# Output projection and gate of a decoder layer: tokens on partitions, seven half-size products, PSUM seeded by VectorE

## The chip, the cores and the metric

The kernel runs on one core of a Trainium2 chip. Its engines work side by side, each through its own queue in order: TensorE (PE, matrix products into PSUM), VectorE (DVE), ScalarE (ACT), GpSimd (POOL), and SyncE (SP), which issues all of this kernel's DMAs. The metric is the device time in microseconds, median of several runs. A profile is one execution, taken by the hardware profiler.

## The reference

One layer over 4096 tokens of 1024 channels, in f32. What is cut away here (convolution, spatial gating) is not touched by the change.

```python
h = _layer_norm(x, ln_emb_g, ln_emb_b)
proj = einsum("bsd,de->bse", h, w_in)                  # 6 parts of 512 channels
y_a = ...  # a = a_val*sigmoid(a_gate); causal depthwise conv of width 31;
           # silu(layer_norm(a)) * silu(a_z)
y_b = ...  # gelu(b_u) * (chunked 128x128 mix of layer_norm(gelu(b_v)) + b_s) * silu(b_z)
y = concatenate([y_a, y_b], axis=-1)                   # 1024 channels
mix = einsum("bse,ed->bsd", y, w_out)                  # output projection
h = _layer_norm(ALPHA * h + mix, post_ln_g, post_ln_b)
pe = einsum("bsk,kd->bsd", p, w_ple)                   # 256 -> 1024
gate = sigmoid(einsum("bsd,de->bse", h, w_ple_gate) + b_ple_gate)
h = h + gate * pe
```

Every f32 product is done in three passes of the fast 32-bit matmul format: an operand is split into a rounded part (hi, by ScalarE) and the rest (lo = source - hi, by VectorE or GpSimd), and hi*hi + lo*hi + hi*lo are summed in PSUM (`mm3`, L158).

## The kernel before, in words

There are eight blocks of 512 tokens and four stages. Stage 1 normalises x, projects the convolution's inputs and its gate, and runs the convolution of channel tiles 0 and 1 on VectorE (`conv`, 31 multiply-adds per tile, L205). Stage 2 (L488) projects the gating branch in three parts of four 128-token tiles per block (L506), mixes it, and runs the convolution of channel tiles 2 and 3 beside it. Intermediate results go to DRAM tensors: `hD` (normalised x), `cD` (convolution), `zD` (silu gate of the first branch), `yD` (second branch).

Stage 3 (L627) is the output projection, with channels on partitions and tokens on the free axis: for each block and each 128 output channels (d), 8 x 3 matmuls of 128x128 by 128x512 go into one PSUM bank (L648). VectorE adds the residual (`zp`, L653), transposes 32x32 pieces and takes moments over channels in groups (L661, L666), which `block_moments` joins through DRAM. `stage_y` (L452) prepares the next block's left side; the eight weights `wO` are split one after the other in stage 2's last block (L554).

Stage 4 (L683) is the gate, in the same layout: `stage_z` (L614) normalises the block's rows, the gate needs 8 x 3 matmuls per 128 output channels (L708), the embedding product 2 x 3 (`embed`, L713), then sigmoid, product, sum and the output's DMA.

Work for later blocks is written as generators (`Background`, L163) from which the loops take a step now and then. The order on each engine is not the written one alone: when the program is built, a scheduler puts every instruction into its engine's queue as soon as its own model of the machine finds its inputs ready, the one written first ahead of others. At run time each queue is strictly in order. Buffers come from pools with a fixed number of tiles under one tag; a tile that is taken again waits for the last user of the old one. All of stages 1 to 4 share the pools `wpool`, `hpool`, `rpool` and `psum` (L60 to L63).

Of the kernel before, what the change touches and what calls it, by code (L numbers as in the profile page):

```python
# [8 lines left out]
F32 = mybir.dt.float32  # L9
# [6 lines left out]
P = 128  # L16
S = 4096
# [17 lines left out]
def hybrid_layer_kernel(  # L35
# [50 lines left out]
    xst = const.tile([P, S // P, 2], F32, name="xst")  # L86
    cw_sb = const.tile([P, CT, W31], F32, name="cw_sb")
# [9 lines left out]
    rD = [dram.tile([KT // 2, P, 2, TB], F32, name=f"rD{b}") for b in range(NB)]  # L97
# [3 lines left out]
    rpD = [dram.tile([4, 32, QT, 12], F32, name=f"rpD{b}") for b in range(NB)]  # L101
    rsD = [dram.tile([32, QT, 2], F32, name=f"rsD{b}") for b in range(NB)]
# [32 lines left out]
    def by_row(eng, dst, src, mr, i):  # L135
        """dst = src - mean (i = 0) or src / deviation (i = 1); tokens on the free axis"""
# [55 lines left out]
    def conv(pairs, dst, part):  # L192
        """pairs: two (channel tile, a tile with its halo) of one block."""
# [29 lines left out]
    # ---------------- phase 1: embedding norm, gate / value / a_z, conv of channel tiles 0, 1  # L223
# [160 lines left out]
    # ---------------- phase 2: b_v, b_u, b_z, spatial gating, conv of channel tiles 2, 3  # L384
# [424 lines left out]
```

## Time and profile before

| | us |
|---|---|
| median of 3 runs (1976.82 to 1980.04) | 1979.33 |
| span of the profiled execution | 1978.5 |
| stage 1, 0 to 569.5 us of the span | 569.5 |
| stage 2, to 1115.9 us | 546.4 |
| stage 3, to 1512.5 us | 396.6 |
| stage 4 | 466.0 |

The span runs from the first to the last instruction; the device time of the profiled execution itself is not listed apart from the runs, whose median lies 0.8 us above the span. The stages are cut where the first matmul of the next one starts (the first with `h_hi`, with `yh`, with `zh`); work of other engines for a later stage may lie before the cut. "Busy" of TensorE counts matmuls, which overlap, so the price of one is read from a stretch without gaps.

### The profile page before, as it was taken

How to read it: one execution, taken by the hardware profiler on the slowest of the kernel's cores; microseconds unless marked ns; L12 is line 12 of the kernel's file. 1: busy time of each engine (PE TensorE's matmuls, PEld its weight loads, DVE VectorE, ACT ScalarE, POOL GpSimd, SP SyncE). 2: the span in 40 equal slices, each digit the busy share in tenths (PEclk: the TensorE clock that was granted, in tenths of full speed). 3: DMA queues.
4: the chain of work that ended last, by engine and by line, in shares of the span. 5: the costliest groups of instructions: out<-in, count | busy, mean ns of one | idle time of the engine just before them, and what ended most of it. 6: DMA issues, size and time to landing. Idle time of an engine off the chain costs nothing.

```text
span 1978.5 us, 23196 instructions
## 1 busy us (share of the span) xinstructions
PE 1892.0 (96%) x8340; PEld 1554.8 (79%) x8340; DVE 1564.5 (79%) x2746; ACT 509.4 (26%) x724; POOL 842.4 (43%) x575
## 2 busy tenths in 40 slices
PE   7999989999999999999999988999897799999999
PEld 6877777878888888888888876778776588888887
DVE  7999998989699999999998576666769766666421
ACT  5323311230332222222222331111202233323321
POOL 1876756461234564655456333332422333323221
PEclk9999999999999999999999999999999899999999
DMA  7644433432321234212223575555535322222111
GB/s 265 210 161 137 153 128 134 126 131 92 130 85 57 68 89 134 67 51 75 66 67 106 169 218 174 175 183 171 173 115 181 120 102 106 101 97 85 59 43 38
DMA packets 176871, 239.44 MB, mean 121 GB/s; under 512 B 21490, under 2 KB 113906, under 8 KB 176756
## 3 DMA queue, kind: packets, MB, share of 16 engines
q1 hardware_dynamic: 176756, 237.96, 37.2%
q8 instruction: 65, 1.06, 0.2%
q14 instruction: 50, 0.41, 0.1%
HBM read 156.55 MB, written 81.36 MB: 120 GB/s over the span
## 4 chain that ended last, share of the span: by engine, by line
PE 55%; DVE 14%; DMA 10%; issue 4%; POOL 3%; ACT 1%; SPq 0%; DVEq 0%; POOLq 0%; ACTq 0%
PE ps L159 11%; PE ps L160 11%; PE ps L161 11%; PE gp L160 5%; PE gp L161 5%; PE gp L159 5%; DVE acc L205 3%; DVE yf L144 2%; DMA zs<-zD 2%; DVE zn L144 2%; PE pp L159 1%; PE pp L161 1%; PE pp L160 1%; DMA rD<-zp 1%; DMA yf<-cD 1%
## 5 line engine op out<-in xcount | busy, mean ns | idle before, releaser
L205 DVE SCALAR_TENSOR_TENSOR acc<-a,cw_sb,acc 128x512 f32<-128x512 f32 x928 | 639.5, 743 | 3.0
L159 PE MATMUL ps<-hh,whi 128*128 128x512 f32 (+1 forms) x784 | 303.7, 390 | 21.0 <-DVE a L336 8.6
L160 PE MATMUL ps<-hl,whi 128*128 128x512 f32 (+1 forms) x784 | 303.8, 388 | 0.8 <-DVE hl L124 0.8
L161 PE MATMUL ps<-hh,wlo 128*128 128x512 f32 (+1 forms) x784 | 303.0, 387 | 0.0
L160 PE MATMUL ps<-wlo,h_hi 128*128 128x512 f32 x768 | 298.9, 389 | 0.0
L159 PE MATMUL ps<-whi,h_hi 128*128 128x512 f32 x768 | 298.9, 389 | 0.0
L161 PE MATMUL ps<-whi,h_lo 128*128 128x512 f32 x768 | 298.8, 389 | 0.0
L696 POOL TENSOR_TENSOR h<-zh,zl 128x512 f32<-128x512 f32 x64 | 116.9, 1830 | 294.7 <-DVE h L727 155.7
L159 PE MATMUL ps<-yh,whi 128*128 128x512 f32 x512 | 205.6, 402 | 31.3 <-DVE zp L653 31.3
L160 PE MATMUL ps<-yl,whi 128*128 128x512 f32 x512 | 203.5, 397 | 0.7 <-POOL yl L124 0.7
L161 PE MATMUL ps<-yh,wlo 128*128 128x512 f32 x512 | 203.4, 397 | 0.0
L160 PE MATMUL gp<-zl,whi 128*128 128x512 f32 x512 | 200.3, 391 | 0.0
L159 PE MATMUL gp<-zh,whi 128*128 128x512 f32 x512 | 200.1, 391 | 0.2 <-DVE zp L653 0.2
L161 PE MATMUL gp<-zh,wlo 128*128 128x512 f32 x512 | 199.7, 390 | 0.0
L159 PEld LDWEIGHTS ps<-hh,whi 128*128 128x128 f32 x784 | 147.6, 189 | 56.5 <-DVE ev L340 10.8
L726 DVE TENSOR_TENSOR sg<-pp,sg 128x512 f32<-128x512 f32 (+1 forms) x65 | 44.3, 683 | 184.2 <-ACT h L700 151.7
L144 POOL TENSOR_TENSOR xk<-xk,mr 128x1024 f32<-128x1024 f32 x42 | 156.7, 3760 | 45.4 <-DMA xk<-in_xT 38.2
L160 PEld LDWEIGHTS ps<-hl,whi 128*128 128x128 f32 x784 | 148.7, 190 | 30.3 <-DVE hl L124 1.2
L161 PEld LDWEIGHTS ps<-hh,wlo 128*128 128x128 f32 x784 | 148.7, 190 | 29.8
L161 PEld LDWEIGHTS ps<-whi,h_lo 128*128 128x128 f32 x768 | 144.2, 188 | 29.8
L159 PEld LDWEIGHTS ps<-whi,h_hi 128*128 128x128 f32 x768 | 144.2, 188 | 29.7
L160 PEld LDWEIGHTS ps<-wlo,h_hi 128*128 128x128 f32 x768 | 144.2, 188 | 29.1
(112 smaller groups left out, 2971.2 us busy)
## 6 DMA issues: line engine op xcount, KB each, us to landing
h_lo<-hD SPq DMA_DIRECT2D x32, 512.0 KB, 3.7
zp<-hD SPq DMA_DIRECT2D x64, 256.0 KB, 3.3
rD<-zp SPq DMA_DIRECT2D x32, 512.0 KB, 4.1
zn<-rD SPq DMA_DIRECT2D x32, 512.0 KB, 4.8
out<-h SPq DMA_DIRECT2D x63, 256.0 KB, 2.0
xt<-in_x SPq DMA_DIRECT2D x28, 512.0 KB, 4.5
xk<-in_xT SPq DMA_DIRECT2D x28, 512.0 KB, 6.4
hD<-xk SPq DMA_DIRECT2D x56, 256.0 KB, 2.5
```

The lines of the kernel that those rows point to most:

```text
L144: eng.tensor_tensor(dst, src, m, op=(ALU.subtract, ALU.mult)[i])
L159: nc.tensor.matmul(ps, lhsT=lh, rhs=rh, start=first, stop=False)
L160: nc.tensor.matmul(ps, lhsT=lh, rhs=rl, start=False, stop=False)
L161: nc.tensor.matmul(ps, lhsT=ll, rhs=rh, start=False, stop=last)
L205: nc.vector.scalar_tensor_tensor(o if t == W31 - 1 else acc, src, w, acc, op0=ALU.mult, op1=ALU.add)
L696: nc.gpsimd.tensor_tensor(h2, zh[e // 2][:, e % 2, :].bitcast(F32), zl[e // 2][:, e % 2, :].bitcast(F32), op=ALU.add,)
L726: nc.vector.tensor_tensor(sg[:, cs], pp[:, cs], sg[:, cs], op=ALU.mult)
```

## The change

Stages 1 and 2 keep their own work. Stages 3 and 4 are written anew, with 128 tokens on partitions and 512 output channels on the free axis, for a pair of 128-token tiles at a time (16 pairs). The left side of a pair is a 2x2 matrix of blocks (two token tiles by two halves of the 1024 inputs), the weight a 2x2 matrix of 512x512 quarters. The 2x2 block product is formed from seven products of sums (Winograd's form of Strassen's scheme) in place of eight. Each product is 4 x 3 matmuls.

The sums on the left (s1 to s4) are made by VectorE in PSUM banks and then split. The sums on the weight's side are made once, beside stages 1 and 2 (`combos`), and kept in the DRAM tensor `twD`. The sums over the products use PSUM's accumulation: several products are added into one bank without starting it anew, and two banks (`pa`, `pd`) are first written by VectorE ("seeded") with an earlier product plus the residual or the bias, and a product is then accumulated on top. `open_banks` runs one matmul with zeros into each of these two banks at the start of stage 3.

The residual alpha*h is prepared beside stage 2 in token layout (`token_rows`, DRAM tensor `hT`). With tokens on partitions the moments of a row are two `bn_stats` and one `bn_aggr`, and ScalarE normalises the row; it goes to DRAM (`zT`), and stage 4 reads it again and transposes it on TensorE (`zn_left`). GpSimd applies gain and offset of the norm to the rows in stage 4. `y_block` prepares a block of the first branch with two of its four channel tiles at a time. Stages 3 and 4 have pools of their own, opened when those of stages 1 and 2 are closed.

```diff
+    psum = p12.enter_context(tc.tile_pool(name="psum", bufs=2, space=PSUM))
...
+    def combos(u, w, scale=None, bias=None):
...
+        for c in range(2):
+            q = {}
+            for i in range(2):
+                for j in range(2):
+                    q[i, j] = b4([P, 2, C], "bq")
+                    dma(q[i, j], w[i, j][:, 2 * c : 2 * c + 2, :])
...
+            for n, ij in ((0, (0, 0)), (1, (1, 0)), (2, (1, 1))):
+                dma(twD[u][n][:, cs, :], q[ij])
+            sub = ALU.subtract
+            nc.gpsimd.tensor_tensor(q[0, 0], q[0, 1], q[0, 0], op=sub)
+            dma(twD[u][4][:, cs, :], q[0, 0])
...
+    def token_rows():
...
+        for tt in range(S // P):
+            xt = b4([P, D], "xrow")
+            dma(xt, x[tt * P : (tt + 1) * P, :])
...
+            nc.gpsimd.tensor_tensor(xt, xt, rows[0], op=ALU.mult)
+            nc.gpsimd.tensor_tensor(xt, xt, rows[1], op=ALU.add)
+            dma(hT[tt], xt)
...
+    bg_row.add(combos(0, wo))
+    bg_row.add(combos(1, wg, dv_sb[:, 2, :], dv_sb[:, 3, :]))
+    bg_row.add(token_rows())
...
+                bg_row.step(1)
-                if b == NB - 1 and part > 0:
-                    d = (part - 1) * JT + j
-                    stg = h4([P, D], "wstg", F32) if part == 1 else q4([P, D], "wstg")
-                    wO[d] = prep_weight(stg, wo[d])
...
+    p12.close()
+    pool = ctx.enter_context(tc.tile_pool(name="p34", bufs=1, reuse_waits="tile"))
+    psum = ctx.enter_context(tc.tile_pool(name="psum34", bufs=1, space=PSUM, reuse_waits="tile"))
...
+    def big(shape, name, dt=F32):
+        return pool.tile(shape, dt, tag="big", name=name, bufs=5)
...
+    def right_operands(u):
+        W = {}
+        for n in ORDER:
+            stg = big([P, 4, C], "wst")
+            dma(stg, twD[u][ROW[n]])
+            hi, lo = wtile("whi"), wtile("wlo")
+            for c in range(2):
+                cs = slice(2 * c, 2 * c + 2)
+                act(hi[:, cs], stg[:, cs], AF.Identity)
+                eng = nc.gpsimd if c else nc.vector
+                eng.tensor_tensor(lo[:, cs], stg[:, cs], hi[:, cs].bitcast(F32), op=SUB)
...
+    def product(ps, n, L, W, start):
+        ah, al = L[n]
+        wh, wl = W[n]
+        kw = dict(skip_group_check=True)
+        for k in range(4):
+            nc.tensor.matmul(ps, lhsT=ah[:, k, :], rhs=wh[:, k, :], start=start and k == 0, stop=False, **kw)
+            nc.tensor.matmul(ps, lhsT=al[:, k, :], rhs=wh[:, k, :], start=False, stop=False, **kw)
+            nc.tensor.matmul(ps, lhsT=ah[:, k, :], rhs=wl[:, k, :], start=False, stop=k == 3, **kw)
...
+    def group(L, W, add11, add12, add21, add22, to12, to22, between):
+        pb = pbank("B", "pb", 2)
+        pe = pbank("E", "pe", 1)
+        product(pb, 1, L, W, True)
+        product(pe, 5, L, W, True)
+        pa = pbank("A", "pa", 1)
+        tt(pa, pb, add11, op=ADD)
+        s5 = utile([P, C], "s5")
+        tt(s5, pe, add22, op=ADD)
+        between(0)
+        product(pb, 6, L, W, False)
+        u2 = utile([P, C], "u2")
+        tt(u2, pb, add12, op=ADD)
+        between(1)
+        product(pe, 3, L, W, False)
+        tt(to12, pe, u2, op=ADD)
+        between(2)
+        product(pb, 7, L, W, False)
+        pd = pbank("D", "pd", 1)
+        tt(pd, pb, add21, op=ADD)
+        tt(to22, pb, s5, op=ADD)
+        between(3)
+        product(pa, 2, L, W, False)
+        between(4)
+        product(pd, 4, L, W, False)
+        between(5)
+        return pa, pd
...
+    def y_block(b):
...
+            by_row(nc.vector, ya[:, us], ya[:, us], mr, 0)
+            by_row(nc.gpsimd, ya[:, us], ya[:, us], mr, 1)
...
+            nc.gpsimd.tensor_tensor(ya[:, us], ya[:, us], zs[:, us], op=ALU.mult)
...
+    def stats(zt, first):
...
+        nc.vector.bn_stats(st[:, 0, :], first)
+        nc.vector.bn_stats(st[:, 1, :], zt[:, C:])
+        nc.vector.bn_aggr(mv[:, 0, :], st)
+        rstd_of(mv)
+        nc.vector.scalar_tensor_tensor(
+            nb, mv[:, 0, 0:1], -1.0, mv[:, 0, 1:2], op0=ALU.mult, op1=ALU.mult
         )
+        for dst, src in ((zt[:, :C], first), (zt[:, C:], zt[:, C:])):
+            act(dst, src, AF.Identity, scale=mv[:, 0, 1:2], bias=nb)
...
+        def between(i):
+            bg.step(2)
+            if i < 2:
+                r = rows[i]
+                nc.gpsimd.tensor_tensor(r, r, gb[:, 0], op=ALU.mult)
+                nc.gpsimd.tensor_tensor(r, r, gb[:, 1], op=ADD)
+            elif i == 3:
+                finish4(0, 1, c12)
+            elif i == 4:
+                finish4(1, 1, c22)
```

In a pair the left operands are made from the blocks a11, a12, a21, a22: s1 = a21 + a22, s2 = s1 - a11, s4 = a12 - s2, s3 = a11 - a21; each is split into `ahi` (ScalarE) and `alo` (VectorE for the four sums, GpSimd for the three plain blocks). `finish4` is sigmoid, embedding product, multiplication, addition and output DMA for half a row tile.

What moves in the queues is shown at three places, each before and after. First GpSimd in a middle block of stage 2. `h_lo` is the rest of the next block's input, `v` and `vl` the normalised value of the gating branch, `mv` its moments, `g` the gated output. Before:

```order
L108 TENSOR_SCALAR mv<-mv 128x1
L124 TENSOR_TENSOR h_lo<-h_lo,h_hi 128x1024
L108 TENSOR_SCALAR mv<-mv 128x1
L109 TENSOR_TENSOR mv<-mv,nhalf 128x1 x2
L521 TENSOR_TENSOR v<-v,sgb 128x512 x2
L108 TENSOR_SCALAR mv<-mv 128x1
L522 TENSOR_TENSOR v<-v,sgb 128x512 x2
```

After, `xrow` being a token row of `token_rows`:

```order
L496 TENSOR_TENSOR xrow<-xrow,hrow 128x1024
L126 TENSOR_TENSOR h_lo<-h_lo,h_hi 128x1024
L495 TENSOR_TENSOR xrow<-xrow,hrow 128x1024
L126 TENSOR_TENSOR h_lo<-h_lo,h_hi 128x1024
L496 TENSOR_TENSOR xrow<-xrow,hrow 128x1024
L495 TENSOR_TENSOR xrow<-xrow,hrow 128x1024
L571 TENSOR_TENSOR g_7310<-g_7310,zz 128x512 x2
L571 TENSOR_TENSOR g_7388<-g_7388,zz 128x512 x2
L496 TENSOR_TENSOR xrow<-xrow,hrow 128x1024
L495 TENSOR_TENSOR xrow<-xrow,hrow 128x1024
L110 TENSOR_SCALAR mv<-mv 128x1
L496 TENSOR_TENSOR xrow<-xrow,hrow 128x1024
```

The token rows stand between the instructions of the gating branch, from block 2 to block 6; in block 1 it is the second set of weight differences. Blocks 0 and 7 of stage 2 have none.

Second, GpSimd where stage 2 ends. Before, the first block's left side (`yf`, `yl`) is mixed with the last gating products:

```order
L470 TENSOR_TENSOR yf<-yf,zs 128x512 [waits DMAHW7_49,Activation_49]
L124 TENSOR_TENSOR yl<-yf,yh 128x512 [waits DMAHW0_49,Activation_49]
L124 TENSOR_TENSOR yl<-yf,yh 128x512 [waits DMAHW1_49,Activation_49]
L534 TENSOR_TENSOR g_8905<-g_8905,zz 128x512 [waits DMAHW3_49,Activation_49]
L124 TENSOR_TENSOR yl<-yf,yh 128x512 [waits DMAHW2_49,PE_49,Activation_49]
L534 TENSOR_TENSOR g_8905<-g_8905,zz 128x512 [waits Activation_49]
```

After, with `g` as above, `zero` the tile of `open_banks`, `ya` the first branch of block 0, `wlo` half a rest of a weight:

```order
L111 TENSOR_TENSOR bmv<-bmv,nhalf 32x16 [waits Pool_49]
L571 TENSOR_TENSOR g_9254<-g_9254,zz 128x512 [waits DMAHW1_49,Activation_49]
L571 TENSOR_TENSOR g_9254<-g_9254,zz 128x512 [waits Activation_49]
L722 MEMSET zero 128x512 [waits PE_49]
L146 TENSOR_TENSOR ya<-ya,mr 128x1024 [waits DMAHW3_49,DMAHW4_49,DVE_49,PE_49]
L146 TENSOR_TENSOR ya<-ya,mr 128x1024 [waits DMAHW5_49,DVE_49]
L784 TENSOR_TENSOR ya<-ya,zs 128x1024 [waits DMAHW6_49,Activation_49,Pool_49]
L784 TENSOR_TENSOR ya<-ya,zs 128x1024 [waits Activation_49,Pool_49]
L659 TENSOR_TENSOR wlo<-wst,whi 128x1024 [waits DMAHW3_49,Activation_49]
L670 TENSOR_TENSOR alo<-ya,ahi 128x512 [waits Activation_49]
```

All of the first block's preparation now stands behind the last product of stage 2, and the first `alo`, which the second matmul of stage 3 waits for, behind a weight's rest.

Third, VectorE in the middle of stage 3. Before, a residual sum frees a bank (`zp`), and transposes, moments and rests of the left side follow:

```order
L653 SCALAR_TENSOR_TENSOR zp<-zp,ps 128x512 [waits PE_49] x2
L661 STREAM_TRANSPOSE zt<-zp 128x512 [waits DVE_49]
L661 STREAM_TRANSPOSE zt<-zp 128x512
L653 SCALAR_TENSOR_TENSOR zp<-zp,ps 128x512 [waits PE_49]
L124 TENSOR_TENSOR yl<-yf,yh 128x512 [waits PE_49,Activation_49]
```

After, from the moments of one row tile to the seeds of the next products (`znb` is -mean/deviation, `pa` and `pd` the seeded banks, `pb` and `pe` the others):

```order
L817 BN_STATS st<-pa 128x6 [waits PE_49]
L819 BN_AGGR zmv<-st 128x2 [waits DVE_49]
L821 SCALAR_TENSOR_TENSOR znb<-zmv 128x1 [waits DVE_49,Pool_49]
L748 TENSOR_TENSOR pd<-pb,row 128x512 [waits PE_49]
L749 TENSOR_TENSOR z_10581<-pb,s_10610 128x512
L735 TENSOR_TENSOR pa<-pb,row 128x512 [waits DMAHW7_49,Activation_49]
L818 BN_STATS st<-z_10581 128x6 [waits DVE_49]
L737 TENSOR_TENSOR s_10772<-pe,row 128x512 [waits DMAHW0_49,PE_49]
```

The seeds now stand behind a VectorE instruction that waits for GpSimd. The order of the products on TensorE in a settled pair is 1, 5, 6, 2, 7, 3, 4.

## Rows read from the trace of the kernel before

**Rows 1.** The page, part 1: busy time, share of the span, instructions
```profile
PE 1892.0 (96%) x8340; PEld 1554.8 (79%) x8340; DVE 1564.5 (79%) x2746; ACT 509.4 (26%) x724; POOL 842.4 (43%) x575
```

**Rows 2.** Windows: length; PE, PEld, DVE, ACT, POOL busy (instructions); clock, DMA share, GB/s
```profile
0.00:569.50 569.50, 538.19 (x2383) 441.34 (x2384) 510.38 (x789) 162.02 (x231) 291.74 (x152) 0.99 0.45 148
569.50:1115.90 546.40, 546.40 (x2501) 456.01 (x2501) 518.87 (x1099) 143.71 (x225) 299.82 (x275) 1.00 0.27 81
1115.90:1512.50 396.60, 364.43 (x1539) 295.08 (x1537) 273.25 (x598) 76.10 (x104) 133.10 (x85) 0.97 0.56 179
1512.50:1978.50 466.00, 442.96 (x1920) 362.38 (x1920) 262.02 (x263) 127.55 (x165) 117.77 (x64) 0.98 0.25 87
1690.00:1960.00 270.00, 270.00 (x1183) 221.57 (x1182) 131.48 (x124) 77.44 (x101) 68.51 (x39) 1.00 0.20 74
```

**Rows 3.** Waits of PE, whole span: in total, times, longest
```profile
PE ps L159 <- DVE zp L653: 31.3, 14, 5.1
PE pp L159 <- ACT ph L123: 13.7, 1, 13.7
```

**Rows 4.** Groups of VectorE by form: busy us, mean ns | idle before
```profile
L144 DVE TENSOR_TENSOR zn<-zn,mr 128x1024 f32<-128x1024 f32 x64 | 133.4, 2121 | 21.8 <-DMA zn<-rD 21.6
L144 DVE TENSOR_TENSOR xk<-xk,mr 128x1024 f32<-128x1024 f32 x14 | 55.7, 3980 | 18.5 <-POOL xk L144 18.5
L726 DVE TENSOR_TENSOR sg<-pp,sg 128x512 f32<-128x512 f32 x63 | 43.5, 691 | 178.3 <-ACT h L700 151.7 <-ACT sg L725 26.6
L124 DVE TENSOR_TENSOR yl<-yf,yh 128x512 fp32r<-128x512 f32 x32 | 25.3, 819 | 33.3 <-ACT yh L123 33.3
L114 DVE BATCH_NORM_STATS2 bst<-v 128x6 f32<-128x512 f32 x32 | 21.7, 679 | 4.2 <-ACT v L516 4.2
L115 DVE BATCH_NORM_AGGREGATE xst<-bst 128x2 f32<-128x12 f32 x32 | 6.4, 200 | 0.1
```

**Rows 5.** Groups of GpSimd by form, the same columns
```profile
L144 POOL TENSOR_TENSOR xk<-xk,mr 128x1024 f32<-128x1024 f32 x42 | 156.7, 3760 | 45.4 <-DMA xk<-in_xT 38.2 <-issue 7.2
L124 POOL TENSOR_TENSOR h_lo<-h_lo,h_hi 128x1024 fp32r<-128x1024 f32 x32 | 77.8, 2433 | 107.1 <-ACT h_hi L123 107.1
L124 POOL TENSOR_TENSOR yl<-yf,yh 128x512 fp32r<-128x512 f32 x32 | 44.2, 1391 | 28.9 <-ACT yh L123 28.8
L109 POOL TENSOR_TENSOR mv<-mv,nhalf 128x1 f32<-128x1 f32 x32 | 18.1, 567 | 1.6
L108 POOL TENSOR_SCALAR mv<-mv 128x1 f32<-128x1 f32 x32 | 8.0, 251 | 33.1 <-DVE mv L115 33.1
```

**Rows 6.** Line 205, convolution: duration min/median/max ns, first and last start
```profile
L205 DVE SCALAR_TENSOR_TENSOR acc<-a,cw_sb,acc x928: 672/745/776, 40.9 to 1068.0; 128x512 f32<-128x512 f32 x186
```

**Rows 7.** PE in order of time, stage 1: start, duration; four transposes
```profile
19.32 0.28 PE L159 MATMUL ps<-hh,whi 128*128 128x256 f32 x1
19.44 0.60 PE L253 MATMUL tp<-ident,xt 128*128 128x128 f32 x4
```

**Rows 8.** A window of the start; GpSimd in order of time, block 1's last rest
```profile
20.00:30.00 10.00, 9.24 (x65) 8.26 (x64) 7.51 (x12) 7.12 (x12) 0.00 (x0) 1.00 1.04 365
...
83.56 2.40 POOL L124 TENSOR_TENSOR hl<-xk,hh 128x1024 fp32r<-128x1024 f32 x1
```

**Rows 9.** GpSimd at the end of stage 2; DMA: count, KB, us to landing
```profile
1120.03 2.93 POOL L109 TENSOR_TENSOR bmv<-bmv,nhalf 32x16 f32<-32x16 f32 x1
1122.94 1.28 POOL L534 TENSOR_TENSOR g<-g,zz 128x512 f32<-128x512 f32 x1
...
wstg<-in_wo SPq DMA_DIRECT2D x8, 512.0 KB, 4.5
mr<-csD SPq DMA_DIRECT2D x8, 512.0 KB, 5.1
```

**Rows 10.** A window behind the wait of stage 4, columns as in rows 2
```profile
1542.00:1546.00 4.00, 3.90 (x9) 3.10 (x10) 4.00 (x6) 0.62 (x2) 0.00 (x0) 0.51 0.61 215
```

**Rows 11.** Tile gp: duration min/median/max ns, first and last start
```profile
L161 PE MATMUL gp<-zh,wlo x512: 388/389/628, 1513.1 to 1973.2; 128*128 128x512 f32 x171
```

More of the change, by code (lines that the diff above doesn't have):

```diff
@@ L414, in cg_prep @@
         ah, al = h4([P, D], "cgh"), h4([P, D], "cgl")
         split(acc, ah, al)
-        for _ in range(8):
+        for _ in range(4):
             yield
@@ new lines, in hybrid_layer_kernel, with zn_left @@
+    Z = {}
+    def zn_left(p, L):
+        Z[p] = load_rows(zT, p)
+        quads = []
+        zq = big([P, 4, 4, P], "zq")
+        for j in range(2):
+            for half in range(2):
+                tp = sbank("tp")
+                for kk in range(4):
+                    k = 4 * half + kk
+                    nc.tensor.transpose(
+                        out=tp[:, kk * P : (kk + 1) * P],
+                        in_=Z[p][j][:, k * P : (k + 1) * P], identity=ident,
+                    )
+                zt = zq[:, 2 * j + half]
+                act(zt, tp.rearrange("p (k x) -> p k x", k=4), AF.Identity)
+                quads.append(zt)
+                yield
+        yield from left_operands(L, *quads, nc.gpsimd)
@@ new lines, in hybrid_layer_kernel @@
+    H = load_rows(hT, 0)
+    for p in range(NP):
+        h1, h2 = H
+        if p + 1 < NP:
+            H = load_rows(hT, p + 1)
+            if p % 2 == 0 and p // 2 + 1 < NB:
+                bg_x.add(y_block(p // 2 + 1))
+            if p % 2 == 1:
+                bg_x.drain()
+            bg.add(left3(p + 1, Lnext))
+        else:
+            bg.add(zn_left(0, Lnext))
+        z1, z2 = ztile([P, D], "z1"), ztile([P, D], "z2")
+        def between(i):
+            bg.step(2)
+            bg_x.step(1)
+        pa, pd = group(
+            L, W, h1[:, :C], h1[:, C:], h2[:, :C], h2[:, C:], z1[:, C:], z2[:, C:], between
+        )
+        stats(z1, pa)
+        dma(zT[2 * p], z1)
+        stats(z2, pd)
+        dma(zT[2 * p + 1], z2)
+        bg.drain()
+        L, Lnext = Lnext, {}
@@ new lines, in hybrid_layer_kernel, with finish4, between @@
+    for p in range(NP):
+        if p + 1 < NP:
+            bg.add(zn_left(p + 1, Lnext))
+        rows = Z.pop(p)
+        ph, pl = p_left(p)
+        c12, c22 = utile([P, C], "c12"), utile([P, C], "c22")
+        def finish4(j, half, src):
+            cs = slice(half * C, (half + 1) * C)
+            sg = c12 if (j, half) == (0, 1) else c22 if (j, half) == (1, 1) else utile([P, C], "sg")
+            act(sg, src, AF.Sigmoid)
+            pp = sbank("pp")
+            ts = slice(j * P, (j + 1) * P)
+            for k in range(2):
+                mm3(
+                    pp, ph[:, k, ts], pl[:, k, ts], wp_hi[:, k, cs], wp_lo[:, k, cs],
+                    k == 0, k == 1,
+                )
+            tt(sg, pp, sg, op=ALU.mult)
+            tt(rows[j][:, cs], rows[j][:, cs], sg, op=ADD)
+            dma(out[2 * p + j][:, cs], rows[j][:, cs])
+        def between(i):
+            bg.step(2)
+            if i < 2:
[6 more added lines that the diff above has]
+                finish4(1, 1, c22)
+        pa, pd = group(L, W, cg[:, :C], cg[:, C:], cg[:, :C], cg[:, C:], c12, c22, between)
+        finish4(0, 0, pa)
+        finish4(1, 0, pd)
+        bg.drain()
+        L, Lnext = Lnext, {}
@@ L737 @@
+_OUT = (S // P, P, D)
 def kernel(**inputs):
```

406 lines of the change are left out of this document (210 added, 196 removed).

## The prediction

> **What bounds the kernel now.** Read the stages first, then the waits of TensorE inside them, then the prices of single instructions. The page gives TensorE 96% of the span, which says only that it is the engine to follow [rows 1]. The windows by stage say more [rows 2]: stage 1 takes 569.5 us and stage 2 546.4 us, and in stage 2 TensorE has no idle time at all, VectorE is 95% busy and GpSimd 55%. Stage 3 takes 396.6 us with TensorE busy 364 us, stage 4 takes 466.0 us with 443 us. A stretch in the middle of stage 4 holds 1183 matmuls in 270 us of unbroken work, so one 128x512 matmul costs 0.228 us when nothing waits. At that price stage 3 (1536 matmuls) is 350 us of work and 46 us of waits and slow clock; stage 4 (1920) is 438 us of work, 5 us behind the last matmul (it starts at 1973.2 us [rows 11]) and 23 us of waits. The named waits are for VectorE's residual sums, which give the accumulators back (31.3 us), and one of 13.7 us at the head of stage 4 [rows 3]. So stages 3 and 4 are bound by TensorE with 69 us of gaps, and stages 1 and 2 share their limit between TensorE and VectorE.
>
> **The change, part by part.** The sum is made against the profiled execution, span 1978.5 us; the median of the runs is 0.8 us above that, which I add at the end.
>
> *Matmuls taken out.* Two blocks of 128 tokens now cost 7 x 12 = 84 matmuls where they cost 96. Over 16 pairs and two stages 384 go: 384 x 0.228 = 88 us. The embedding product keeps its 384.
>
> *Transposes put in.* The normalised rows come back with tokens on partitions and are transposed on TensorE, 16 per pair in stage 4. Four of them lasted 0.60 us at full clock, where a single short matmul beside them shows 0.28 us [rows 7], so one adds (0.60 - 0.28) / 3 = 0.107 us; 256 make 27 us. Net saving 61 us.
>
> *Stage 3 per pair.* TensorE 84 x 0.228 = 19.2 us, 306 us for 16. VectorE, with prices from [rows 4]: two sums with both inputs in SBUF at 0.819, twelve sums and rests with an input in PSUM at 0.691, four moments at 0.679, four small ones at about 0.2, one subtraction of row means at 2.12: 15.6 us. GpSimd [rows 5]: three rests at 1.39, one multiplication by the row deviations at 3.76, one by the gate at 2.43, two powers with their addition at 0.82: 12.0 us. TensorE is still the longest, but the margin to VectorE is 3.6 us. Three times in a pair a product waits for a VectorE sum over the product that ended one place earlier, so with a cover of 12 x 0.228 = 2.7 us. In the third piece of order the statistic behind `BN_AGGR zmv` is waited for by VectorE itself, on GpSimd: 0.82 us at least, up to 3.76 us more if a long GpSimd instruction has just begun, and the seed `pd<-pb` and then `pa<-pb` are queued behind it on VectorE; products 4 and 6 wait for those two. Bounds: 0.3 us per pair (the unbroken 270 us of stage 4 show that such a structure can run without gaps) and 4 us (VectorE's 15.6 us and two such waits of 3.8 us: 23.2 us). I take 1.5 us, nearer to the row without gaps: 24 us.
>
> *One price that could be higher.* The row-mean subtraction takes 2.12 us where GpSimd is quiet and 3.98 us in stage 1, where GpSimd multiplies the same kind of tile at the same time [rows 4]. The convolution's steps, with one SBUF stream and the accumulator in PSUM, stay between 672 and 776 ns all through stages 1 and 2 [rows 6]. The Trainium skill (SBUF — State Buffer, "Who interferes with whom") has the rule: a VectorE instruction with two SBUF inputs contends with a GpSimd one that reads SBUF, one with a single SBUF input does not. By the rule, and the trace agrees, the seeds and sums over PSUM escape GpSimd, and the row-mean subtraction, which the change runs beside GpSimd's, does not. At 3.98 us VectorE's pair goes from 15.6 to 17.5 us; my sum has this inside the 1.5 us of waits.
>
> *Stage 4 per pair.* TensorE 84 + 24 matmuls and 16 transposes: 24.6 + 1.7 = 26.3 us, 421 us for 16. VectorE 16.2 us (twenty-one instructions at 0.691, two sums at 0.819 [rows 4]), GpSimd 3 x 1.39 + 4 x 2.43 = 13.9 us: both well below. Three PSUM banks now serve twelve small users per pair (sums, transposes, embedding). Bounds 0 (no gap in the 270 us) and 3 us per pair (a bank each time held for one rest, one copy and one product); I take 0.9 us: 14 us.
>
> *From stage 2 to stage 3.* Before, the first product of stage 3 begins 0.4 us after the last of stage 2, because inputs and weights were prepared under stage 2. Now the first y block is loaded behind the last `yD` writes on SP and prepared with TensorE idle. Step by step from the end of stage 2's matmuls: the last gating multiplication ends at 1124.2 us, 8.3 us late, behind a long power [rows 9]; its transposes, taken as one sum, 0.69; the row moments landing 5.1 [rows 9]; means 2.1; two deviations on GpSimd 7.5; two gate multiplications 4.9; then, by the second piece of order, half a weight rest 2.4 and the first operand's rest 1.4: 32 us. Seven weights of 1 MB follow through two or three free buffers at some 9 us a load (512 KB take 4.5 [rows 9]), and GpSimd has six more rests of 2.4 us and six of 1.4 us, done 23 us after the first product may start; two pairs hold 38 us of products, so most of this is covered: I add 8 us, with 1.6 us of half clock in it (after the 13.7 us wait of stage 4 the granted clock was 0.51 [rows 10]). Together 40 us, bounds 25 (the loads slip ahead) and 60 (every weight waited for).
>
> *From stage 3 to stage 4.* The seven gate weights take the buffers that the last pair gives back, one product apart. VectorE does 7 x 1.3 us more in that pair: 8 us, bounds 3 and 20.
>
> *Stage 2.* GpSimd gets the token rows (64 instructions) and the second set of weight differences (16), all 128x1024 at 2.43 us [rows 5]: 195 us. Its work was 299.8 / 8 = 37.5 us per block of 68.3 us. By the order nearly all of it lies in blocks 1 to 6: 225 + 195 = 420 us in 410 us of TensorE. So GpSimd becomes as long as TensorE there, in a fixed order, with the next block's `h_lo` rests and VectorE's `mv` behind the token rows. Bounds: 0 (blocks 0 and 7 take up the 10 us) and 56 (GpSimd reaches 90%: 420 / 0.9 = 466). I take 18.
>
> *Start.* Eight weight loads and fourteen writes of 512 KB, 11 MB, move in among the first loads. From 20 to 30 us the DMA engines are full at 365 GB/s, and block 1's last rest ends at 86 us [rows 8], when TensorE is already on block 1: no slack. 11 MB are 30 us of transfer at that rate, most of it in free slots: 8 us, bounds 0 and 25.
>
> *Sum.* 1115.9 + 8 + 18 + 40 + 306 + 24 + 8 + 421 + 14 + 5 = 1960 us; with 0.8 us, **1961 us**, 0.9% below 1979.33. In short: 61 us of TensorE's work and 69 us of old gaps go, 112 us of new ones come.
>
> **Rivals.** *Everything hides.* Stage 1 and 2 keep their times, the step to stage 3 costs 25 us, the pairs wait 0.3 us: 1116 + 25 + 306 + 5 + 3 + 421 + 5 + 1 = 1882 us. For it: the long stretch without gaps. Against it: the GpSimd chain of 32 us, whose parts are all measured.
> *GpSimd bounds stage 2 (slower).* Place: blocks 1 to 6. Price: 56 us in place of 18, so 1999 us. It decides from 37 us on, when GpSimd reaches no more than 94% of its time there. For it: 420 us of work in 410. Against: in stage 2 GpSimd idles 45% of the time before [rows 2], and blocks 0 and 7 are left to catch up in.
> *VectorE bounds stage 3.* A pair takes 23.2 us in place of 20.7: 41 us more, 2002 us. It is also the case in which seeding by VectorE undoes what seven products save. For it: the statistic that VectorE waits for in its own queue, and the 3.98 us price. Against: the 2.7 us cover at each of the three places.
>
> **How the numbers follow.** The forecast's own case, 1930 to 1985 us, gets 0.45, the hidden one 0.26, GpSimd in stage 2 0.15, VectorE in stage 3 0.14. This kernel's measurement can tell about 0.2% (4 us) from no change. Of the forecast's 0.45, 0.36 lies more than that below, 0.07 within and 0.02 above; of the GpSimd case 0.01 within. Faster 0.36 + 0.26 = 0.62, same 0.08, slower 0.02 + 0.14 + 0.14 = 0.30. The range that leaves out 2 in 10 cuts into both sides: 1895 to 2020 us.
>
> **What would show it.** Right: 7,926 matmuls besides transposes in place of 8,308 and a busy TensorE near 1,800 us; an idle TensorE of about 32 us at the end of stage 2, ended by a GpSimd rest; stage 3 pairs of 20 to 21 us, with `pa`, `pd` and `pb` waits for VectorE of 1 to 2 us a pair; stage 4 pairs near 27 us; GpSimd over 85% busy in the middle of stage 2. Wrong: a stage 2 longer than 590 us, a stage 3 pair over 23 us, or waits for a PSUM bank in stage 4 of more than 3 us a pair. A first product of stage 3 within 10 us of stage 2's end would make the hidden case true.

## The result and the profile after

The change made the kernel slower: 2006.44 us (median of 4 runs, 2001.65 to 2009.85) against 1979.68 us before, a ratio of 1.0133 (95% interval 1.011 to 1.0156). The forecast was 1961 us, faster; the measured time lies inside the stated range of 1895 to 2020 us, on the other side of the kernel before.

The profiled execution has a span of 1999.9 us. Its page, part 1, answers to [rows 1]:

```profile
PE 1856.2 (93%) x8214; PEld 1523.2 (76%) x8214; DVE 1603.6 (80%) x2645; ACT 643.5 (32%) x969; POOL 1242.5 (62%) x784
```

TensorE has 126 instructions and 36 us of busy time less and still ends later; GpSimd has 400 us more. Windows by stage say where, with the columns of [rows 2]. The five stretches are stage 1, stage 2 to its last projection, the step to the first product, stage 3 to the last product of its 16th pair, and stage 4; then four settled pairs of stage 3 and ten of stage 4:

```profile
0.00:581.20 581.20, 547.33 (x2385) 447.40 (x2386) 518.73 (x790) 162.71 (x232) 310.15 (x160) 0.98 0.49 168
581.20:1162.70 581.50, 553.74 (x2501) 460.25 (x2499) 525.79 (x1104) 169.76 (x242) 477.97 (x350) 0.97 0.40 134
1162.70:1190.90 28.20, 1.45 (x4) 0.54 (x3) 7.33 (x5) 6.25 (x9) 14.31 (x7) 0.55 0.87 302
1190.90:1555.90 365.00, 330.56 (x1384) 267.17 (x1384) 270.81 (x375) 151.05 (x226) 201.26 (x150) 0.95 0.55 194
1555.90:1999.90 444.00, 423.07 (x1945) 347.87 (x1944) 280.90 (x374) 153.71 (x262) 238.85 (x119) 0.98 0.28 91
1457.00:1533.00 76.00, 76.00 (x337) 62.94 (x336) 46.85 (x87) 28.42 (x44) 21.25 (x28) 1.00 0.36 125
1700.00:1960.00 260.00, 260.00 (x1227) 216.00 (x1226) 157.88 (x225) 90.02 (x158) 136.26 (x70) 1.00 0.28 88
```

| us | before | forecast | after |
|---|---|---|---|
| stage 1 | 569.5 | 577.5 | 581.2 |
| stage 2 | 546.4 | 564.4 | 581.5 |
| step to stage 3 | 0 | 32 | 28.2 |
| stage 3 | 396.6 | 338 | 365.0 |
| stage 4 and tail | 466.0 | 448 | 444.0 |

Where the new stages run settled they do what the count says: four pairs of stage 3 in 76 us, 19.0 us each (84 matmuls), and stage 4 in 26 us a pair, both with no idle TensorE and the clock at 1.00. What is lost against the forecast is lost ahead of that. The waits of TensorE, over the span (total, times, longest), answer to [rows 3]:

```profile
PE pb L715 <- ACT ahi L669: 25.5, 2, 24.2
PE pb L715 <- DVE pa L735: 20.0, 5, 6.0
PE ps L470 <- POOL ones L464: 19.5, 1, 19.5
...
PE pb L715 <- DVE u L741: 8.2, 4, 3.2
PE sp L161 <- DVE g L606: 7.3, 3, 3.9
```

The first is nearly all the step to stage 3 (24.2 us). The third lies in the middle of stage 2, in work that the forecast had passed over. Line 470 sums the gate's bias over its weights with a left side of ones. TensorE there, in order of time:

```profile
820.72 0.39 PE L163 MATMUL ps<-whi,h_lo 128*128 128x512 f32 x1
840.58 1.22 PE L470 MATMUL ps<-cgh,ones 128*128 128x512 f32 x2 [19.47 <-POOL ones L464]
841.60 0.63 PE L161 MATMUL ps<-whi,h_hi 128*128 128x512 f32 x1
```

And GpSimd up to the fill that it waits for:

```profile
833.84 2.34 POOL L496 TENSOR_TENSOR xrow<-xrow,hrow 128x1024 f32<-128x1024 f32 x1
836.15 0.56 POOL L111 TENSOR_TENSOR mv<-mv,nhalf 128x1 f32<-128x1 f32 x1
836.68 1.40 POOL L126 TENSOR_TENSOR vl<-v,vh 128x256 fp32r<-128x256 f32 x2
838.05 2.33 POOL L496 TENSOR_TENSOR xrow<-xrow,hrow 128x1024 f32<-128x1024 f32 x1
840.33 0.20 POOL L464 MEMSET ones<- 128x128 f32 x1
```

A fill of 0.2 us, which waits for nothing but its turn, holds TensorE for 19.5 us; the matmuls behind it last 0.63 us in place of 0.39 (from 841.6 to 844.2 us the granted clock was 0.50, the lower of its two levels).

The pairs of stage 3 (from one pair's last product to the next one's) took 45.2, 26.1, 24.7, 21.5, 19.0, 24.2, 19.0, 27.6, 13.3, 26.8 us, then five of 19.0 and 22.4 at the end. These stretches do not all hold 84 product matmuls, since products of the next pair run ahead of a pair's last: the first holds 120, the second 72, the eighth to tenth 97, 59 and 96. Against 19.0 us each, the first pair is 26 us longer, pairs 1 to 9 (counted from 0) 31 us, pairs 10 to 14 nothing. Counted by matmuls at the settled price (19.0 us for 84), the first loses 18 us and pairs 1 to 9, which hold 744 in place of 756, lose 34. What happens at the loss in pair 1, on GpSimd, VectorE and TensorE:

```profile
1237.97 2.35 POOL L784 TENSOR_TENSOR ya<-ya,zs 128x1024 f32<-128x1024 f32 x1
```
```profile
1238.04 2.29 DVE L821 SCALAR_TENSOR_TENSOR znb<-zmv 128x1 f32<-128x1 f32 x1 [0.94 <-POOL zmv L111]
...
1241.17 0.70 DVE L735 TENSOR_TENSOR pa<-pb,row 128x512 f32<-128x512 f32 x1 [0.85 <-ACT z L825]
```
```profile
1241.93 0.79 PE L715 MATMUL pb<-whi,ahi 128*128 128x512 f32 x1 [5.81 <-DVE pa L735]
```

`znb` has one element per partition; its median is 160 ns. Here it lasts 2.29 us and ends at 1240.33, with GpSimd's instruction (1240.32). ScalarE's normalisation waits for it, the seed `pa` for that, and TensorE for the seed. Ten of the 32 `znb` took over 0.5 us, and each of them ended within 0.02 us of a GpSimd instruction. The Trainium skill (SBUF — State Buffer, "Who interferes with whom") says that a VectorE instruction with two SBUF inputs contends with a GpSimd one that reads SBUF, for a pair of ports that is an exclusive lock; this trace agrees, down to the common end.

### The profile page after: what moved, and what is told of

The parts are those of the page before. It is cut to its first block, busy times and chain, and to the rows that moved or that the text cites. A ratio compares the mean times of both kernels' runs of the same rounds, so it can differ in the third digit from the quotient of the medians.

```text
span 1999.9 us, 23511 instructions
## 1 busy us (share of the span) xinstructions
PE 1856.2 (93%) x8214; PEld 1523.2 (76%) x8214; DVE 1603.6 (80%) x2645; ACT 643.5 (32%) x969; POOL 1242.5 (62%) x784
## 5 line engine op out<-in xcount | busy, mean ns | idle before, releaser
L715 PE MATMUL pb<-whi,ahi 128*128 128x512 f32 x384 | 157.7, 412 | 54.6 <-ACT ahi L669 25.5
L146 POOL TENSOR_TENSOR xk<-xk,mr 128x1024 f32<-128x1024 f32 x42 | 150.2, 3603 | 47.0 <-DMA xk<-in_xT 26.5
L162 PEld LDWEIGHTS ps<-hl,whi 128*128 128x128 f32 x784 | 150.6, 192 | 31.6 <-DVE hl L126 1.8
L716 PE MATMUL pb<-whi,alo 128*128 128x512 f32 x384 | 154.8, 403 | 0.7 <-POOL alo L670 0.7
L717 PE MATMUL pb<-wlo,ahi 128*128 128x512 f32 x384 | 154.3, 402 | 0.3 <-DVE wlo L659 0.3
L926 POOL TENSOR_TENSOR row<-row,gb 128x1024 f32<-128x1024 f32 x32 | 84.3, 2640 | 99.7 <-PE tp L839 93.8
L715 PEld LDWEIGHTS pb<-whi,ahi 128*128 128x128 f32 x384 | 75.0, 195 | 74.9 <-ACT ahi L669 26.7
L669 ACT ACTIVATE ahi<-s 128x512 fp32r<-128x512 f32 x128 | 76.0, 596 | 142.4 <-DVE s L694 35.2
L715 PE MATMUL pe<-whi,ahi 128*128 128x512 f32 x256 | 104.1, 406 | 12.7 <-DVE s L737 7.0
L670 DVE TENSOR_TENSOR alo<-s,ahi 128x512 fp32r<-128x512 f32 x128 | 87.0, 684 | 26.2 <-ACT ahi L669 19.0
```

Of the source, the lines that this page charges most:

```text
L146: eng.tensor_tensor(dst, src, m, op=(ALU.subtract, ALU.mult)[i])
L162: nc.tensor.matmul(ps, lhsT=lh, rhs=rl, start=False, stop=False)
L669: act(view(hi), src, AF.Identity)
L670: eng.tensor_tensor(view(lo), src, view(hi).bitcast(F32), op=SUB)
L715: nc.tensor.matmul(ps, lhsT=ah[:, k, :], rhs=wh[:, k, :], start=start and k == 0, stop=False, **kw)
L716: nc.tensor.matmul(ps, lhsT=al[:, k, :], rhs=wh[:, k, :], start=False, stop=False, **kw)
```

## The experiments

Stretches of the profiled executions in us; "first" is the first pair of stage 3, "1 to 9" what pairs 1 to 9 took above 171 (nine of 19.0); the first stretch holds 120 matmuls, but 108 in e7, f3, f4 and f5, which moves 2.7 us from "first" to "1 to 9"; the ratio is to the kernel before, from several runs (two for h1).

| kernel | median | ratio, interval | S1 | S2 | step | S3 | S4 | first | 1 to 9 |
|---|---|---|---|---|---|---|---|---|---|
| changed | 2006.4 | 1.0133, 1.011–1.0156 | 581.2 | 581.5 | 28.2 | 365.0 | 444.0 | 45 | 31 |
| e1 | 1989.7 | 1.0075, 1.0048–1.0102 | 580.4 | 567.1 | 28.2 | 369.0 | 443.0 | 44 | 37 |
| e2 | 1991.1 | 1.0076, 1.0056–1.0097 | 568.4 | 580.8 | 28.0 | 365.0 | 445.4 | 45 | 32 |
| e4 | 2014.0 | 1.0185, 1.0164–1.0206 | 579.1 | 589.2 | 30.2 | 370.8 | 444.2 | 39 | 44 |
| e7 | 2001.2 | 1.0128, 1.0103–1.0152 | 581.7 | 589.1 | 28.0 | 365.6 | 435.8 | 38 | 40 |
| f1 | 1977.2 | 0.9991, 0.9978–1.0003 | 568.0 | 563.7 | 27.9 | 369.4 | 444.1 | 45 | 36 |
| f2 | 1970.4 | 0.9962, 0.9949–0.9976 | 570.3 | 570.9 | 24.9 | 366.3 | 444.8 | 37 | 41 |
| f3 | 1961.1 | 0.9909, 0.9893–0.9925 | 568.8 | 565.6 | 24.8 | 364.0 | 436.1 | 35 | 42 |
| g1 | 1975.8 | 0.9989, 0.9969–1.001 | 581.0 | 556.1 | 28.7 | 361.5 | 445.3 | 44 | 28 |
| h1 | 1966.8 | 0.994, 0.9922–0.9959 | 581.9 | 587.4 | 28.1 | 329.8 | 438.1 | 44 | 0 |
| h2 | 1978.6 | 0.9998, 0.9978–1.0018 | 576.9 | 587.0 | 28.1 | 347.7 | 437.5 | 40 | 20 |
| f4 | 1968.6 | 0.9969, 0.9946–0.9991 | 567.5 | 565.6 | 22.0 | 370.9 | 436.2 | 43 | 39 |
| f5 | 1967.1 | 0.9964, 0.995–0.9978 | 566.9 | 564.0 | 25.6 | 364.9 | 438.7 | 35 | 42 |

The changed kernel, e4 and e7 have the same queues in stage 2 and took 581.5, 589.2 and 589.1 us there, so some 8 us of that stage can differ without a cause in the queues. Each row's stretches are those of one execution.

**e1_ones_early**

```diff
-        ones = rpool.tile([P, P], F32R, tag="e", name="ones", bufs=4)
-        nc.gpsimd.memset(ones.bitcast(F32), 1.0)
+        ones = nhalf.bitcast(F32R)
```

> The two matmuls that sum the gate's bias use, as their left side, a constant of -0.5 that is there from the start (and VectorE multiplies by -2) in place of a tile of ones that GpSimd fills late. Theory A (TensorE stands 19.5 us in stage 2 only because this fill has its place in GpSimd's full queue): the wait goes, stage 2 falls from 581 to about 561 us, and the time from 2006 to about 1985 us. Rival B (GpSimd has too much work in stage 2, and the same time is lost at the next thing that it feeds): stage 2 stays above 575 us, the time above 2000 us.

Stage 2 fell to 567.1 us, not to 561. What remains is one more wait at the same matmul, now for its right side (`cgh`):

```profile
PE ps L469 <- ACT cgh L125: 6.3, 1, 6.3
```

Theory A holds for the wait, with 14 of 20 us; stage 3 was 4 us longer in this execution.

**e2_combos_late**

```diff
                     q[i, j] = b4([P, 2, C], "bq")
+                    if u == 0 and c == 0:
+                        act(q[i, j][:, 0, 0:1], hs[0][0][:, 0, 0:1].bitcast(F32), AF.Identity)
```

> The first set of weight differences cannot start before the first rows of stage 2 are loaded (one element of each of the first four tiles is written from them), so that its loads leave the start of the program and run at the end of stage 1, where GpSimd is idle three quarters of the time. Theory A (stage 1 is 11.7 us longer because of these loads and differences): stage 1 comes back to 570 us, stage 2 stays at 581, the time falls by 9 to 12 us to about 1996 us. Rival B (stage 1 is longer because the whole order came out otherwise): stage 1 stays above 577 us and the time at 2003 to 2010 us.

Stage 1 is back at 568.4 us, stage 2 unchanged: theory A. The edit moves the loads and the differences made from them together, so the two are not told apart. The window of stage 1, against the first of the changed kernel, has 8 us less of busy TensorE for the same matmuls and a higher clock:

```profile
0.00:568.40 568.40, 538.91 (x2384) 441.50 (x2385) 508.94 (x786) 162.46 (x235) 314.92 (x160) 0.99 0.51 171
```

**g1_no_row_gain**

```diff
-            nc.gpsimd.tensor_tensor(xt, xt, rows[0], op=ALU.mult)
-            nc.gpsimd.tensor_tensor(xt, xt, rows[1], op=ALU.add)
```

> The changed kernel without gain and offset of the residual's rows: 64 GpSimd instructions of 128x1024, 155 us, are left out of stage 2. Theory A (GpSimd's full queue is what lengthens stage 2: 19.5 us by the tile of ones behind it, some 14 us by everything else that is late): stage 2 falls from 581 to 550 us or less, and TensorE's waits there to under 5 us. Rival B (the matmuls with ones and the half clock behind them cost this whatever GpSimd has to do): stage 2 stays above 565 us.

Stage 2 alone, without these rows on GpSimd (325 us busy in place of 478):

```profile
581.00:1137.10 556.10, 550.23 (x2501) 458.23 (x2499) 515.39 (x1104) 170.49 (x242) 325.29 (x286) 0.99 0.41 140
```

TensorE idles 5.9 us in place of 27.8, and the wait for the tile of ones is gone too. The stage falls to 556.1 us, between the two forecasts and nearer to theory A. So GpSimd's full queue costs some 25 us there, the late tile included. The 10 us above before's 546.4 may lie with the second set of differences and the bias sums, which stay; that was not tested.

**e4_rows_vector**

```diff
-            by_row(nc.gpsimd, ya[:, us], ya[:, us], mr, 1)
+            by_row(nc.vector, ya[:, us], ya[:, us], mr, 1)
```

> In the preparation of the first branch's blocks the multiplication by the row deviations goes from GpSimd to VectorE (16 instructions of 128x1024). Theory A (VectorE instructions with both inputs in SBUF and GpSimd instructions shut each other out, which stretches VectorE's to 2.3 to 4 us in the first ten pairs of stage 3): two such instructions in a row on VectorE cost 2.0 us each, fewer GpSimd instructions are left to wait for, and pairs 1 to 9 lose some 10 us of their 31 us above 19.0: about 1996 us. Rival B (VectorE is simply full there): 33 us more on VectorE over these blocks, the odd pairs get 2 to 3 us longer: about 2020 us.

Pairs 1 to 9 lost 13 us more. Theory A's forecast failed here, though its premise held: in these pairs the row instructions took 2.08 us, s1 and s3 0.69 and `znb` 0.29 by their means, where the changed kernel has 2.41, 0.90, 1.06 and 0.84. TensorE now waits 22.3 us there for the sum `u` of VectorE, which often has two row instructions, 4 us together, close ahead of it in the queue; the prediction's cover was 2.7 us. So VectorE's own work in a fixed order can cost as much as the exclusion, nearer to rival B.

**e7_rests_vector**

```diff
-                eng = nc.gpsimd if c else nc.vector
+                eng = nc.vector
```

> The rests of the seven weights of stage 3 and of the gate are all made by VectorE (fourteen halves at 1.6 to 2 us per set) in place of half by VectorE and half by GpSimd at 2.4. Theory A (VectorE and GpSimd shut each other out in these instructions, so that sharing them out gains nothing): the first pair of stage 3 falls from 45 to about 38 us and the step to the gate by some us: about 1997 us. Rival B (the two halves run beside each other): VectorE gets 7 x 1.6 = 11 us more in the first pair, 52 to 56 us in place of 45: about 2016 us.

VectorE's rests by form, stages 3 and 4's start (columns as in [rows 4]); the changed kernel, then this one:

```profile
L659 DVE TENSOR_TENSOR wlo<-wst,whi 128x1024 fp32r<-128x1024 f32 x10 | 26.7, 2678 | 9.9 <-ACT whi L657 9.9
```
```profile
L659 DVE TENSOR_TENSOR wlo<-wst,whi 128x1024 fp32r<-128x1024 f32 x18 | 27.5, 1548 | 9.8 <-ACT whi L657 9.8
```

Eighteen take as long as ten did: beside GpSimd's half VectorE's half had waited for much of its time. The first pair gained 8 us and stage 4 another 8; pairs 1 to 9 gave 9 back, most of it in pair 1 (37.5 us), and stage 2 was 8 us longer without cause in its queues. VectorE is busy for 36.8 of the first pair's 37.5 us (41.2 of 45.2 in the changed kernel), so it is full or nearly full there either way. The time is the same within the interval.

**h1_no_pool_rows and h2_no_vector_rows** test pairs 1 to 9, from the changed kernel.

```diff
 # h1
+            if b == 0:
                 by_row(nc.gpsimd, ya[:, us], ya[:, us], mr, 1)
...
+            if b == 0:
                 nc.gpsimd.tensor_tensor(ya[:, us], ya[:, us], zs[:, us], op=ALU.mult)
 # h2
+            if b == 0:
                 by_row(nc.vector, ya[:, us], ya[:, us], mr, 0)
```

> The changed kernel without GpSimd's part of preparing the first branch's blocks 1 to 7 (multiplication by the row deviations and by the gate left out: 28 instructions, 79 us of GpSimd). VectorE's part stays. Theory A (in pairs 1 to 9 VectorE's two-input instructions are stretched because GpSimd's long ones shut them out): VectorE's row instructions fall to 2.0 us each, the sums s1 and s3 to 0.69, and pairs 1 to 9 lose more than 15 of their 31 us above 19.0 each. Rival B (VectorE's own load of row means, weights' rests and sums in a fixed order is the cause): pairs 1 to 9 lose under 8 us.

> The changed kernel without VectorE's part of preparing the first branch's blocks 1 to 7 (the subtraction of the row means left out: 14 instructions, 34 us of VectorE). GpSimd's part stays. Theory A (GpSimd's long instructions shut VectorE's two-input ones out): GpSimd still holds VectorE up, pairs 1 to 9 lose under 12 of their 31 us. Rival B (VectorE's own load): they lose more than 20 us.

Windows of pairs 1 to 9: the changed kernel, h1, h2:

```profile
1236.10:1438.30 202.20, 179.54 (x746) 145.55 (x746) 154.12 (x213) 82.10 (x128) 120.60 (x89) 0.95 0.54 185
```
```profile
1241.50:1412.10 170.60, 169.15 (x746) 139.48 (x745) 134.39 (x214) 81.54 (x127) 56.49 (x63) 1.00 0.64 222
```
```profile
1232.20:1423.60 191.40, 175.07 (x746) 142.92 (x746) 129.66 (x203) 83.98 (x130) 116.18 (x90) 0.96 0.59 203
```

Without GpSimd's part the nine pairs run at 19.0 us in the mean and the clock stays at 1.00; VectorE's row subtractions are all still there. Without VectorE's part 20 of the 31 us remain, though VectorE is busy for less time than in h1 (129.7 us against 134.4). Theory A. The changed kernel is 31.6 us longer than h1 here; 21 of that are idle TensorE (22.7 us against 1.5) and 10 are clock: as many matmuls are busy 179.5 us in place of 169.2, at a mean granted clock of 0.95. VectorE's groups of stage 3 in h1:

```profile
L146 DVE TENSOR_TENSOR ya<-ya,mr 128x1024 f32<-128x1024 f32 x16 | 33.9, 2132 | 13.4 <-DMA ya<-cD 11.0 <-issue 2.4
L688 DVE TENSOR_TENSOR s<-yb,ya 128x512 f32<-128x512 f32 x16 | 13.0, 816 | 0.0
L702 DVE TENSOR_TENSOR s<-ya 128x512 f32<-128x512 f32 x16 | 12.1, 757 | 0.0
```

In the changed kernel the means were 2422, 955 and 961 ns.

h1 takes GpSimd's instructions out, and with them two ways to hold VectorE up: the exclusion, and the wait for a power that stands behind them in GpSimd's queue. The traces tell these apart. In pairs 1 to 9 VectorE waited 13.4 us for these powers in the changed kernel and 11.8 us in h1, nearly the same; but its instructions, as many (213 and 214), were busy for 154.1 us and 134.4. So here the loss comes with the stretched instructions. In h2 both are there: 30.1 us of waits for powers, and `znb`, s1 and s3 still at 0.84, 1.23 and 0.98 us.

**f1_both** is e1 and e2 together.

> Both edits that helped: the bias sums without the late tile of ones, and the first set of weight differences kept out of the program's start. Theory A (two separate losses, one of TensorE waiting in stage 2, one of loads in stage 1): they add, stage 1 at 569 and stage 2 at 567 us, the time 23 us below the changed kernel, at 1975 to 1980 us, level with the kernel before. Rival B (one and the same lack of GpSimd's time, found at two places): the second gives back part, 1985 to 1992 us.

The two add: theory A, level with the kernel before.

**f2_early_y** adds a step to stage 2's last block:

```diff
+    def early_y():
+        mr = b4([P, TB, 2], "mr")
...
+            by_row(nc.vector, t, t, mr, 0)
+            by_row(nc.gpsimd, t, t, mr, 1)
...
+            dma(yaD[:, us], t)
```

> As f1_both, and the first branch of block 0 is finished inside stage 2's last block, on idle GpSimd and VectorE, and passed to stage 3 through DRAM. Theory A (the 28 us before stage 3 are a chain: output transposes, SP's writes, loads, row means, deviations, gate, rest): without the middle of the chain the first product begins 19 us after stage 2 in place of 28, the first pair is 2 to 3 us shorter, and the time falls by 10 to 12 us to about 1966 us. Rival B (the first pair waits for its weights whatever comes ahead of it): the first product begins earlier and the first pair gets longer by the same, the time stays at 1975 to 1980 us.

Half of it: against f1 the step fell by 3 us, not 9, the first pair by 8, and pairs 1 to 9 gave 5 back. The median is 6.8 us lower; the profiled execution, at 1978.9 us, was the longest of its twelve. In this kernel and the next the step ends with the first weight's rounding by ScalarE, behind operands whose loads (`yb`, `ya`) follow the last writes of stage 2; TensorE's two waits in f3:

```profile
1145.36 1.22 PE L753 MATMUL seed<-zero 128*128 128x512 f32 x2 [10.77 <-POOL zero L749]
1159.24 0.79 PE L742 MATMUL pb<-whi,ahi 128*128 128x512 f32 x1 [12.66 <-ACT whi L684]
```

**f3_early_y_rests** is f2 and e7.

> As f2_early_y, and all rests of weights on VectorE. Theory A (VectorE's instructions with two SBUF inputs and GpSimd's shut each other out; in the first test of this the gain of 8 us in the first pair was given back in the second, where block 1's preparation came late): stage 4's first pairs gain 8 us as in that test, the first pair of stage 3 some us, the second gives back less than there: 8 to 12 us below f2_early_y. Rival B (VectorE's load decides in the first two pairs): they get 3 to 4 us longer together and only stage 4's 8 us stay, 4 us below f2_early_y.

The median is 9.2 us below f2's, theory A's size. The profiled executions lie further apart (17.9 us, 5.3 of them in stage 2, where the two kernels do the same); in stage 4 they differ by 8.7 us, where both theories had 8, and in stage 3 by 2.3. The first two pairs of stage 3 got 3 us longer together, as rival B has it, and the next two 9 us shorter; so the two are not told apart here. At 0.9909 (0.9893 to 0.9925) of the kernel before it is the fastest of all: with its surroundings mended the change gains 0.9%.

**f4_early_w** splits the first weight inside stage 2 and issues the last writes by two queues.

```diff
+        hi = [b4([P, 2, C], "w1h", F32R) for _ in range(2)]
+        lo = [b4([P, 2, C], "w1l", F32R) for _ in range(2)]
...
-            dma(ya, yaD)
+            nc.scalar.dma_start(ya, yaD)
```

> As f3_early_y_rests, and the first of the seven weights is split inside stage 2's last block (its four buffers are kept through all stages), the last output writes of stage 2 and the loads of block 0 are issued by two queues. Theory A (24.8 us before stage 3 are now a chain of writes, loads and the first weight's rounding): the first product begins 14 us after stage 2, the first pair falls from 34 to about 32 us, and the time by 10 to 14 us, to about 1949 us. Rival B (seven weights' loads and rests set the end of the first two pairs whenever they start): the gap shrinks but the first two pairs get longer by the same, the time stays at 1957 to 1961 us.

The step fell by 3 us and the first pair grew by 9; the first two together took 73.6 us for 72.6. That is nearer to rival B, but the time, 1968.6 us (1960.9 to 1985.3), is above both forecasts, and the test is not clean: the loads that ScalarE now issues stand in its queue ahead of the roundings (those of `yb` from 1145.5 to 1154.3 us, with the first operand's rounding right behind them).

**f5_halves** cuts blocks 1 to 7's preparation into pieces half as long.

```diff
-            by_row(nc.vector, ya[:, us], ya[:, us], mr, 0)
-            by_row(nc.gpsimd, ya[:, us], ya[:, us], mr, 1)
+            for k in (2 * u, 2 * u + 1):
+                by_row(nc.vector, ya[:, k], ya[:, k], mr, 0)
+                by_row(nc.gpsimd, ya[:, k], ya[:, k], mr, 1)
```

> As f3_early_y_rests, and the preparation of blocks 1 to 7 of the first branch is cut into instructions of 128x512 in place of 128x1024, on VectorE and GpSimd alike: the same work in twice as many pieces. Theory A (the two engines shut each other out, and what a product waits for is the length of one GpSimd instruction that a VectorE one meets): waits are halved where the cover of 2.7 us was just missed, pairs 1 to 9 lose 8 to 15 of their 42 us above 19.0, the time falls to about 1950 us. Rival B (the sum of both engines' exclusive work decides, not its pieces): pairs 1 to 9 stay within 5 us, the time at 1957 to 1965 us.

Pairs 1 to 9 stay at 42 us: rival B, though the time, 1967.1 us, is just above its range. Shorter pieces did not help here; taking GpSimd's work out did, in h1.

## Why the prediction was wrong

The saving was right in its count: 7,926 matmuls, settled pairs of 19.0 us in stage 3, stage 4 within 4 us of its sum (some 7 us of its work already lie in stage 3's stretch). TensorE's busy time came out at 1856.2 us and not near 1,800; the mean granted clock fell from 0.986 to 0.965. The step to stage 3 was 28.2 us for 32: in the changed kernel it is the chain that was forecast, but without its middle, the row work, only 3 us went (f2), since the first weight was ready hardly earlier. Stage 1 lost 11.7 us for 8, from the loads named there and the differences made from them (e2). Two terms hold the error of 40 us, 44 together; the others take 4 off.

*Stage 2, 35 us for 18.* The step that failed first is "I take 18", worked out as GpSimd's 420 us of work against 410 us of TensorE. GpSimd was in fact full:

```profile
920.00:990.00 70.00, 69.62 (x319) 57.78 (x318) 64.05 (x136) 24.81 (x36) 68.73 (x49) 1.00 0.50 171
```

But what the sum lacked was not throughput: while GpSimd was full in this window, TensorE was busy for 69.6 of 70 us. One TensorE instruction of the change itself, in the middle of unrelated products, waited 19.5 us for a small GpSimd instruction at the end of that queue. The forecast named what stands behind the token rows (`h_lo`, VectorE's `mv`) and left out `combos`' own matmul. With that wait gone (e1) 14 us go and the stage takes 567.1 us, close to the 564.4 of the forecast; with the rows gone (g1) 25. The other 11 us go with the rows' work, or lie in the 8 us by which this stage differs without a cause in its queues; no run tells these apart.

*Stage 3, 27 us more.* The sum had 24 us of waits, 1.5 in every pair, and 8 for the first weights. The step that failed here is "I take 1.5 us", with the 8 us of the first weights. Instead the settled pairs wait for nothing; the first is 26 us longer, 8 of them work for pair 1, with VectorE busy for 41.2 of its 45.2 us and seven weights' rests stretched by GpSimd's half (e7); and pairs 1 to 9 lose 31. Why the first two pairs together do not get shorter when these rests do (71.3 us in the changed kernel, 75.0 in e7) stays open. The mechanism was named: the statistic queued on VectorE behind GpSimd, and the Trainium skill's rule on two SBUF inputs (SBUF — State Buffer, "Who interferes with whom"). VectorE's waits for GpSimd's powers were no more than foreseen, 13.4 us in pairs 1 to 9; h1, which loses nothing there, has 11.8. The exclusion was mis-sized in two ways. It was priced at one instruction, the row-mean subtraction (3.98 for 2.12 us), "inside the 1.5 us of waits"; it also strikes `znb`, s1, s3 and the weights' rests, and it strikes where the scheduler bunches the preparation of seven blocks into the first ten pairs. And waits are paid again in clock: after the 5.81 us wait shown above TensorE's matmuls last 0.63 us, at a granted clock of 0.50 (1242 to 1246 us), and by the windows above 10 of the 31 us are clock. The rival "VectorE bounds stage 3" had the place and nearly the size (41 us), by another road: in pairs 1 to 9 VectorE is busy for 154 of 202 us, and its instructions are stretched by GpSimd's, as h1 shows. e4 shows the rival's own road: with the stretch gone and VectorE's load raised, more is lost.

## What to carry to other kernels

Work that goes to an idle engine is paid by whoever waits behind it in order; look for every short instruction of the change on that engine that a busy engine waits for, and put constants ahead of the rush. Before giving half of an elementwise job to GpSimd, see how many of VectorE's instructions beside it take two SBUF inputs, for then the two halves may run one after the other; but moving the work to VectorE helps only where a product's cover leaves room for it (e4). Code that is written for later but needs only free buffers can be pulled into a program's start, where the loads are full.

## Not expected of the hardware

The exclusion works the other way too, and over several instructions: GpSimd's 128x1 addition lasted 4.57 us while VectorE ran three two-input instructions back to back (2.04, 0.68, 2.07 us, to 1379.71), and ended 0.1 us after the third; before the change 32 such instructions took 0.25 us in the mean [rows 5]. GpSimd, then VectorE:

```profile
1375.24 4.57 POOL L110 TENSOR_SCALAR zmv<-zmv 128x1 f32<-128x1 f32 x1 [6.23 <-DVE zmv L819]
```
```profile
1375.07 2.04 DVE L146 TENSOR_TENSOR ya<-ya,mr 128x1024 f32<-128x1024 f32 x1
1377.04 0.68 DVE L688 TENSOR_TENSOR s<-yb,ya 128x512 f32<-128x512 f32 x1
1377.64 2.07 DVE L146 TENSOR_TENSOR ya<-ya,mr 128x1024 f32<-128x1024 f32 x1
```

The price of the exclusion here does not follow the size of the instruction that waits: `znb`, 160 ns by its median, reached 2.83 us, and ended within 0.02 us of the GpSimd instruction beside it.
